# Attention scores as three fp32r passes over stored high and low parts of query and key

## The chip, the cores and the metric

The kernel runs on one core of one Trainium2 chip. The metric is the device time of one execution in microseconds (us); lower is better. TensorE is called PE, its weight loads PEld, VectorE DVE, ScalarE ACT, GpSimd POOL and SyncE SP. In this kernel nearly every DMA is issued from SP's queue, which works in order.

## The reference, cut to what matters

One layer of a decoder: a modulated norm, one input projection, two groups of heads side by side (a gated delta rule and a sparse attention), an output projection and a SwiGLU feed-forward part, for a prompt of 2048 tokens and for 8 sample rows. All arrays are float32. The part that the change touches is the prompt's sparse attention, with 4 query heads, 2 key heads and 128 channels:

```python
def block(xs):                                   # 128 queries at a time
    q_b, iq_b, iw_b, t0 = xs
    score = _index_scores(iq_b, ik, iw_b)        # 8 small indexer heads
    score = jnp.where(key_pos[None, None, :] <= qpos[None, :, None], score, -jnp.inf)
    _, idx = lax.top_k(score, topk)              # 256 keys for each query
    ...
    return _attend_selected(q_b, ks, vs, valid)  # softmax(q k / sqrt(d)) v over those keys
```

The kernel does not gather. For a block of 128 queries it forms the scores against all keys up to the block's end, adds a bias that is about -1e30 where a key was not selected, and takes the softmax over the row.

## The kernel before, in words

The work on the prompt is cut into 4 groups of 512 tokens (`g`) and 16 blocks of 128 queries (`i`). The first phase projects the four groups and runs the delta rule. The second runs the feed-forward part (`ffn`, groups 0 to 3), attention for blocks 4 to 15 (`index`, `attend`) and the sample rows (`sample_gdn`, `sample_steps`) beside each other. Blocks 0 to 3 go through `first_attn` in the first phase, in buffers that the delta rule lends.

**Two kinds of matmul.** The projections and the feed-forward part are made of `mm3`: each operand is held as a high part, rounded to the format fp32r, and a low part, the rest, and three fp32r matmuls (high by high, high by low, low by high; lines L184, L185 and L186) add up in one bank. The scores of attention (L1766) are a single matmul on float32 operands, which the trace shows as two MATMUL records. The indexer's dot products (L1721) are pairs of fp32r matmuls.

**Attention of a block.** `attend` loads the block's query `qT` once (L1755). For each of the 2 key heads and each chunk of up to 512 keys it loads `kT` (L1762), and for each of the 2 query heads it makes one score matmul into a bank of the tag `s` (two banks in all). One DVE instruction (L1767) adds the bias, keeps the running maximum and frees the bank. A block `i` has `(i+1)*128` keys, so the chunks of the 16 blocks over the 4 heads make 160 score matmuls: 112 of 512 columns and 16 each of 384, 256 and 128. Then come the exponential on ACT, transposes (L1795), products with V (L1783) and a store.

**Where query and key come from.** `tok` turns a projected block by PE transposes (L990 for the query, L1004 for the key) into a bank `s`; ACT copies it to a tile `qo` (L996, 512 columns; L1014, 256 columns); SP stores it to `qT_d` or `kT_d` in DRAM. `qo` comes from the tag `m`, 8 buffers shared by many small tiles.

**The buffers in the second phase.** `kT` and `V` have `KR` = 3 buffers of 128x512 each, `qT` one, and the sample rows' work tiles `s2` have `S2` = 8. The last feed-forward group borrows attention's tiles for its split weights: `pair()` gives, in turn, a buffer of `wi` (`WI` = 3, both parts) and a pair of one `kT` and one `V` tile.

**What sets the order.** PE's order is written by a planner (`weave`, `step`): each stage is a generator that yields what it costs on PE, how long to wait, and which banks it uses. `MM` = 0.23 is the price of an fp32r matmul of 512 columns, `F4` = 0.88 that of a float32 one. The feed-forward part runs when the other work's spent PE time has reached `PACE` times its own progress (`share`). PE's instructions are tied together as written; those of the other engines and of SP's queue are placed by a scheduler.

Of the kernel before, what the change touches and what calls it, by code (L numbers as in the profile page):

```python
# [34 lines left out]
T = 2048  # L35
# [18 lines left out]
OB = 1  # L54
KR = 3
RB = 2
WR, WI = 2, 3
S2, S4, LATE = 8, 1044, 8000
MM, TP, F4, LAG, EARLY, PACE, GONE_BY = 0.23, 0.46, 0.88, 0.6, 3000, 463, 1e9
# [53 lines left out]
class K:  # L113
# [106 lines left out]
    def build(self):  # L220
        tc, nc = self.tc, self.nc
        with ExitStack() as es:
            self.cp = self.pool(es, "cp")
            self.dr = self.pool(es, "dr", space=bass.MemoryType.DRAM)
            self.oT_d = [self.dr.tile([8, 128, T], F32, name=x) for x in ("oTh_d", "oTl_d")]
            self.qT_d = self.dr.tile([NB, 128, H * 128], F32, name="qT_d")
            self.iqT_d = self.dr.tile([NB, 128, 8 * 128], F32, name="iqT_d")
            self.kT_d = self.dr.tile([2, 128, T], F32, name="kT_d")
            self.V_d = self.dr.tile([T, 256], F32, name="V_d")
            self.ikT_d = self.dr.tile([2, 128, T], F32, name="ikT_d")  # L230
            self.cT_d = self.dr.tile([NB, 128, 12, 128], F32, name="cT_d")
            self.gz_d = self.dr.tile([NB, 128, 512], F32, name="gz_d")
            self.ikp_d = self.dr.tile([NS // 2, 128, NPAGE, 2, 64], F32, name="ikp_d")
            self.kp_d = self.dr.tile([NS, 128, NPAGE, 256], F32, name="kp_d")
            self.vp_d = self.dr.tile([NS, 128, NPAGE, 256], F32, name="vp_d")
            self.gc_d = self.dr.tile([NG, 16, 128], F32, name="gc_d")
            self.gates = {b: self.dr.tile([D], F32, name=f"gate{b}") for b in (16, 40)}
            self.x2_d = self.dr.tile([T, D], F32, name="x2_d")
            self.ps = self.pool(es, "ps", space=PSUM)


            self.p, self.wp = self.pool(es, "p"), self.pool(es, "w")
            with ExitStack() as e1:
                self.phase1(e1)
            if self.stages < 2:
                return
            with ExitStack() as e2:
                self.phase2(e2)
# [727 lines left out]
    def tok(self, what, blk, a, rows):  # L976
# [8 lines left out]
        if what == "aq":  # L985
# [5 lines left out]
            if samp:  # L991
                nc.scalar.copy(self.qTs, pt[:, :32].rearrange("p (h n) -> p h n", h=H))
                yield 0.1, 0
                return
            q = self.m("qo")[:, :512]
            nc.scalar.copy(q, pt)  # L996
            nc.sync.dma_start(self.qT_d[blk], q)
            yield TP, 0
        elif what == "kv":
# [6 lines left out]
            if samp:  # L1006
# [5 lines left out]
                return  # L1012
            q = self.m("qo")[:, :512]
            nc.scalar.copy(q[:, :256], pt[:, :256])  # L1014
            nc.sync.dma_start(self.kT_d[:, :, tk].rearrange("h p n -> p h n"), q[:, :256].rearrange("p (h n) -> p h n", h=2))
            nc.sync.dma_start(self.V_d[tk], a[:, 256:512])
# [3 lines left out]
        else:  # L1020
# [16 lines left out]
            for b in range(2):  # L1037
# [11 lines left out]
                yield TP, 0  # L1049


    def inverse(self, NT, slot):
# [626 lines left out]
    def buffers(self):  # L1679

        p = self.p2
        one = lambda tag, w, bufs=1, dt=F32: lambda: p.tile([128, w], dt, name=tag, tag=tag, bufs=bufs)
        return dict(pool=p, kT=one("kT", 512, KR), V=one("V", 512, KR), ikT=self.ikT, qT=one("qT", 512), iqT=one("iqT", 1024), sc=one("sc", T + 18, 2),
                    bias=one("bias", T, 2, BF), big=one("big", T, 2), rl=one("rl", 512, 2),
                    PT=one("PT", 512, 2), oT=one("oT", 512, OB))

    def first_attn(self, i0):
# [4 lines left out]
        if i0:  # L1692
            for a in range(2):
                ikT.append(p.tile([128, GT], F32, name="gzc", tag="gzc", bufs=2))
                nc.sync.dma_start(ikT[a], self.ikT_d[a, :, :GT])
        B = dict(pool=p, kT=one("E"), V=one("AT"), ikT=ikT, qT=one("qe"), iqT=one("sq", 1024), sc=lambda: p.tile([128, 528], F32, name="ct", tag="ct", bufs=4),
                 bias=one("dec", 512, BF), big=one("Dm"), rl=one("decb"), PT=one("Y"), oT=one("v"))
# [52 lines left out]
    def attend(self, i, B, bias):  # L1750
        nc, p = self.nc, B["pool"]
        n = (i + 1) * 128
        chunks = self.widths(n)
        qT = B["qT"]().rearrange("p (h n) -> p h n", h=H)
        nc.sync.dma_start(qT, self.qT_d[i].rearrange("p (h n) -> p h n", h=H))  # L1755
        st = p.tile([128, 4, 8], F32, name="st", bufs=2)
        oT = B["oT"]().rearrange("p (h n) -> p h n", h=H)
        for kv in range(2):
            Ps = [B["big"]() for _ in range(2)]
            for c, w in chunks:  # L1760
                kT = B["kT"]()
                nc.sync.dma_start(kT[:, :w], self.kT_d[kv, :, c * 512:c * 512 + w])  # L1762
                for r in range(2):
                    h = kv * 2 + r
                    ps = self.ps.tile([128, 512], F32, name="s", tag="s", bufs=2)
                    self.o(nc.tensor.matmul(ps[:, :w], qT[:, h, :], kT[:, :w], start=True, stop=True))  # L1766
                    nc.vector.tensor_tensor_reduce(Ps[r][:, c * 512:c * 512 + w], ps[:, :w], bias[:, c * 512:c * 512 + w], 1.0,  # L1767
                                                   GONE if c == 0 else st[:, h, c - 1:c], OP.add, OP.max, st[:, h, c:c + 1])
                    yield F4 * w / 512, 0, dict(dve=0.2 + 0.6 * w / 512, use="s", need="s")
            for r in range(2):  # L1770
# [68 lines left out]
    def ffn(self, g):  # L1839
# [51 lines left out]
        def pair():  # L1891
            ring[0] += 1
            if ring[0] % 2:
                w = wp.tile([128, 2, 512], F32R, name="wi", tag="wi", bufs=WI)
                return w[:, 0], w[:, 1]
            return [q.tile([128, 512], F32R, name=tag, tag=tag, bufs=KR) for tag in ("kT", "V")]

# [270 lines left out]
```

## Time and profile before

| | |
|---|---|
| times of three runs | 3600.11, 3608.34, 3610.41 us; median 3608.34 |
| the profiled execution | 3607.71 us, span of its instructions 3605.8 us, mean granted clock 0.971 |
| busy, of the span | PE 93%, PEld 72%, DVE 59%, ACT 41%, POOL 16% |
| DMA | 549.60 MB, mean 152 GB/s; SP's queue 47.7% of the 16 engines' time |

A row of the groups names the line, the engine, the operation, the tiles as out<-in, the shape and the count; then, after the bar, the time in which at least one of the group ran, the mean duration of one in ns, and the engine's idle time before them with what ended it. In order of time a row is the start, the duration, the engine, the line and the tiles. A matmul's duration reaches past the start of the next, so the cost of one is read from start to start.

### The profile page before, as it was taken

How to read it: one execution, taken by the hardware profiler on the slowest of the kernel's cores; microseconds unless marked ns; L12 is line 12 of the kernel's file. 1: busy time of each engine (PE TensorE's matmuls, PEld its weight loads, DVE VectorE, ACT ScalarE, POOL GpSimd, SP SyncE). 2: the span in 40 equal slices, each digit the busy share in tenths (PEclk: the TensorE clock that was granted, in tenths of full speed). 3: DMA queues.
4: the chain of work that ended last, by engine and by line, in shares of the span. 5: the costliest groups of instructions: out<-in, count | busy, mean ns of one | idle time of the engine just before them, and what ended most of it. 6: DMA issues, size and time to landing. Idle time of an engine off the chain costs nothing.

```text
span 3605.8 us, 60166 instructions
## 1 busy us (share of the span) xinstructions
PE 3362.7 (93%) x21994; PEld 2601.9 (72%) x21994; DVE 2122.1 (59%) x4502; ACT 1472.4 (41%) x2855; POOL 593.4 (16%) x539
## 2 busy tenths in 40 slices
PE   8899989989997988999998999999899999899997
PEld 5667767767775767777766777777677777677775
DVE  5555635645743656666767655666766654554545
ACT  4333322422433333444456455454545643332323
POOL 1000001100000113222220121222112112222223
PEclk9999999999998999999999999999999999999999
DMA  8754764665686244455354344335433333522221
GB/s 287 241 185 157 224 232 145 219 221 175 212 274 212 92 143 126 140 165 164 122 200 140 119 148 152 102 105 194 138 95 108 98 102 103 181 76 82 78 83 57
DMA packets 421013, 549.60 MB, mean 152 GB/s; under 512 B 50020, under 2 KB 287817, under 8 KB 420698
## 3 DMA queue, kind: packets, MB, share of 16 engines
q1 hardware_dynamic: 420690, 545.62, 47.7%
q8 instruction: 175, 2.87, 0.3%
q14 instruction: 132, 1.08, 0.1%
q10 hardware_dynamic: 16, 0.03, 0.0%
HBM read 441.78 MB, written 122.70 MB: 157 GB/s over the span
## 4 chain that ended last, share of the span: by engine, by line
PE 53%; DVE 6%; issue 3%; ACT 2%; DMA 2%; SPq 1%; POOL 1%; DVEq 0%; ACTq 0%; POOLq 0%
PE d L184 13%; PE d L186 13%; PE d L185 12%; PE s L1721 3%; PE s L1766 3%; PE g L1783 3%; PE g L1795 1%; DVE wi L168 1%; PE g L200 1%; PE g L201 1%; DMA wr<-in_w_ffn_in_dram 1%; DMA wr<-in_w_out_dram 1%; ACT bias L1590 1%; ACT wi L167 0%; DVE ca L1857 0%
## 5 line engine op out<-in xcount | busy, mean ns | idle before, releaser
L184 PE MATMUL d<-hh,wi 128*128 128x512 f32 x1616 | 694.8, 430 | 26.5 <-DVE tm L1857 6.3
L185 PE MATMUL d<-hl,wi 128*128 128x512 f32 x1616 | 643.8, 398 | 5.3 <-DVE hl L489 5.1
L168 DVE TENSOR_TENSOR wi<-wr,wi 128x512 fp32r<-128x512 f32 x525 | 396.1, 755 | 419.6 <-ACT wi L167 413.9
L186 PE MATMUL d<-hh,wi 128*128 128x512 f32 x1616 | 643.0, 398 | 0.0
L167 ACT CAST wi<-wr 128x512 fp32r<-128x512 f32 x525 | 324.4, 619 | 702.4 <-PE d L186 396.4
L184 PEld LDWEIGHTS d<-hh,wi 128*128 128x128 f32 x1616 | 310.6, 192 | 122.4 <-issue 21.0
L185 PEld LDWEIGHTS d<-hl,wi 128*128 128x128 f32 x1616 | 311.2, 193 | 75.8 <-issue 10.1
L186 PEld LDWEIGHTS d<-hh,wi 128*128 128x128 f32 x1616 | 310.0, 192 | 69.8 <-DVE wi L168 0.4
L184 PE MATMUL d<-wi,hh 128*128 128x512 f32 x736 | 317.3, 431 | 19.1 <-DMA wi<-kept 11.5
L185 PE MATMUL d<-wi,hh 128*128 128x512 f32 x736 | 292.2, 397 | 0.4 <-DVE wi L168 0.4
L186 PE MATMUL d<-wi,hl 128*128 128x512 f32 x736 | 291.7, 396 | 0.3 <-issue 0.3
L184 PE MATMUL d<-wi,ah 128*128 128x512 f32 x616 | 263.4, 428 | 9.2 <-ACT ah L2102 5.4
L2103 POOL TENSOR_TENSOR al<-ca,ah 128x512 fp32r<-128x512 f32 x88 | 121.8, 1394 | 907.0 <-ACT ah L2102 906.8
L186 PE MATMUL d<-wi,al 128*128 128x512 f32 x616 | 245.2, 398 | 2.5 <-POOL al L2103 2.5
L185 PE MATMUL d<-wi,ah 128*128 128x512 f32 x616 | 244.2, 396 | 0.0
L1730 DVE SCALAR_TENSOR_TENSOR sc<-rl,iw,sc 128x512 f32<-128x512 f32 (+3 forms) x224 | 174.9, 781 | 75.0 <-ACT rl L1723 69.0
L1723 ACT ACTIVATE rl<-s 128x512 f32<-128x512 f32 (+3 forms) x288 | 151.4, 543 | 151.7 <-PE s L1721 127.5
L1858 POOL TENSOR_TENSOR xt<-xt,tm 128x512 f32<-128x512 f32 x96 | 141.2, 1482 | 401.3 <-DVE tm L1857 339.3
L184 PEld LDWEIGHTS d<-wi,hh 128*128 128x128 f32 x736 | 140.7, 191 | 64.1 <-DMA wi<-kept 16.2
L1590 ACT ACTIVATE bias<-sc,sv 128x640 bf16<-128x640 f32 (+11 forms) x120 | 169.9, 1416 | 35.7 <-DVE sv L1592 22.9
L1721 PE MATMUL s<-ik,iqT 128*128 128x512 f32 (+3 forms) x576 | 170.6, 392 | 9.2 <-DMA iqT<-iqT_d 4.9
L186 PEld LDWEIGHTS d<-wi,hl 128*128 128x128 f32 x736 | 140.5, 191 | 32.2 <-issue 0.3
(570 smaller groups left out, 5952.8 us busy)
## 6 DMA issues: line engine op xcount, KB each, us to landing
wi<-kept SPq DMA_DIRECT2D x168, 512.0 KB
wr<-in_w_ffn_in_dram SPq DMA_DIRECT2D x584, 128.0 KB
wr<-in_w_ffn_out_dram SPq DMA_DIRECT2D x148, 256.0 KB
kept<-wi SPq DMA_DIRECT2D x56, 512.0 KB
row<-in_w_ada_dram SPq DMA_DIRECT2D x32, 512.0 KB
wr<-in_w_in_dram SPq DMA_DIRECT2D x56, 256.0 KB
xt<-in_x_prompt_dram SPq DMA_DIRECT2D x7, 2048.0 KB
kT<-kT_d SPq DMA_DIRECT2D x54, 256.0 KB
```

What stands on the lines that cost most here:

```text
L167: nc.scalar.copy(hi, wr)
L168: nc.vector.tensor_tensor(lo, wr, hi.bitcast(F32), op=OP.subtract)
L184: self.o(nc.tensor.matmul(out, wh, xh, start=start, stop=False, **kw))
L185: self.o(nc.tensor.matmul(out, wh, xl, start=False, stop=False, **kw))
L186: self.o(nc.tensor.matmul(out, wl, xh, start=False, stop=stop, **kw))
L1590: nc.scalar.activation(c, s, AF.Sign, bias=t, accum_out=cnt)
L1721: self.o(nc.tensor.matmul(ps[:, :w], iq[:, h, :].bitcast(F32R), B["ikT"][c * 2 + a][:, :w].bitcast(F32R), start=a == 0, stop=a == 1))
L1723: nc.scalar.activation(r[:, :w], ps[:, :w], AF.Relu)
L1730: nc.vector.scalar_tensor_tensor(s, r[:, :w], iw, s, op0=OP.mult, op1=OP.add)
L1766: self.o(nc.tensor.matmul(ps[:, :w], qT[:, h, :], kT[:, :w], start=True, stop=True))
L1858: (nc.vector if soon else nc.gpsimd).tensor_tensor(xt, xt, tm, op=OP.add)
L2103: nc.gpsimd.tensor_tensor(al[b], a, ah[b].bitcast(F32), op=OP.subtract)
```

## The change

Query and key are split when they are stored, and the scores become `mm3`. `parts` takes the place of the copy in `tok`: ACT casts the bank to fp32r, DVE subtracts to get the rest, and two tiles `qo` are stored by two DMAs. `qT_d` and `kT_d` hold both parts, `attend` loads both by two DMAs, and the score is three fp32r matmuls. To make room, `kT` has 2 buffers of both parts (`RK`) in place of 3 of one, `qT` one buffer of twice the size, and `s2` 6 buffers in place of 8. The borrowed weight pair becomes one `kT` buffer, of which there are 2, where it was one `kT` and one `V`, of which there were 3. In the first phase `first_attn` takes the tags `NT` and `kd` for the low parts. The planner's cost of a score falls from `F4` to `3 * MM`.

```diff
-S2, S4, LATE = 8, 1044, 8000
+RK = 2
+S2, S4, LATE = 6, 1044, 8000
...
-            self.qT_d = self.dr.tile([NB, 128, H * 128], F32, name="qT_d")
+            self.qT_d = self.dr.tile([NB, 128, 2, H * 128], F32, name="qT_d")
...
-            self.kT_d = self.dr.tile([2, 128, T], F32, name="kT_d")
+            self.kT_d = self.dr.tile([2, 128, 2, T], F32, name="kT_d")
...
-            q = self.m("qo")[:, :512]
-            nc.scalar.copy(q, pt)
-            nc.sync.dma_start(self.qT_d[blk], q)
+            for e, q in enumerate(self.parts(pt, 512)):
+                nc.sync.dma_start(self.qT_d[blk, :, e], q)
...
+    def parts(self, pt, w):
+        nc = self.nc
+        hi, lo = [self.m("qo", F32R)[:, :w] for _ in range(2)]
+        nc.scalar.copy(hi, pt[:, :w])
+        nc.vector.tensor_tensor(lo, pt[:, :w], hi.bitcast(F32), op=OP.subtract)
+        return hi.bitcast(F32), lo.bitcast(F32)
...
-        return dict(pool=p, kT=one("kT", 512, KR), V=one("V", 512, KR), ikT=self.ikT, qT=one("qT", 512), ...
+        two = lambda tag, bufs: lambda: (lambda x: [x[:, 0], x[:, 1]])(p.tile([128, 2, 512], F32R, name=tag, tag=tag, bufs=bufs))
+        return dict(pool=p, kT=two("kT", RK), V=one("V", 512, KR), ikT=self.ikT, qT=two("qT", 1), ...
...
-        B = dict(pool=p, kT=one("E"), V=one("AT"), ikT=ikT, qT=one("qe"), ...
+        two = lambda *tags: lambda: [p.tile([128, 512], F32R, name=tag, tag=tag, bufs=2) for tag in tags]
+        B = dict(pool=p, kT=two("E", "NT"), V=one("AT"), ikT=ikT, qT=two("qe", "kd"), ...
...
-                nc.sync.dma_start(kT[:, :w], self.kT_d[kv, :, c * 512:c * 512 + w])
+                for e in range(2):
+                    nc.sync.dma_start(kT[e][:, :w].bitcast(F32), self.kT_d[kv, :, e, c * 512:c * 512 + w])
...
-                    self.o(nc.tensor.matmul(ps[:, :w], qT[:, h, :], kT[:, :w], start=True, stop=True))
+                    self.mm3(ps[:, :w], *[x[:, h * 128:(h + 1) * 128] for x in qT], *[x[:, :w] for x in kT], True, True)
...
-                    yield F4 * w / 512, 0, dict(dve=0.2 + 0.6 * w / 512, use="s", need="s")
+                    yield 3 * MM * w / 512, 0, dict(dve=0.2 + 0.6 * w / 512, use="s", need="s")
...
-            return [q.tile([128, 512], F32R, name=tag, tag=tag, bufs=KR) for tag in ("kT", "V")]
+            w = q.tile([128, 2, 512], F32R, name="kT", tag="kT", bufs=RK)
+            return w[:, 0], w[:, 1]
```

How the order of the instructions changes is shown at three places. In the changed kernel the lines are shifted: `mm3` is L185, L186 and L187 there, the weights' loads are L167, the key's loads L1773.

The first place is PE in the second phase, at block 15, second key head: `s<-kT,qT` are scores, `d<-...` the feed-forward part's matmuls. Before:

```order
L1766 MATMUL s<-kT,qT 128x512 x2
L184 MATMUL d<-hh,wi 128x512
L185 MATMUL d<-hl,wi 128x512
L186 MATMUL d<-hh,wi 128x512
L1766 MATMUL s<-kT,qT 128x512 x2
```

The same place in the changed kernel:

```order
L185 MATMUL s<-kT,qT 128x512
L186 MATMUL s<-kT,qT 128x512
L187 MATMUL s<-kT,qT 128x512
L185 MATMUL s<-kT,qT 128x512
L186 MATMUL s<-kT,qT 128x512
L187 MATMUL s<-kT,qT 128x512
L185 MATMUL d<-hh,wi 128x512
L186 MATMUL d<-hl,wi 128x512
L187 MATMUL d<-hh,wi 128x512
```

Two float32 matmuls have become six fp32r ones, and the feed-forward part's groups of three stand between the chunks as before.

The second place is SP's queue at the same block: `kT<-kT_d` are the key's loads, `wr<-...` the feed-forward weights' that stand among them. Before:

```order
L166 DMA wr<-in_w_ffn_in_dram 128x256 x8
L1762 DMA kT<-kT_d 128x512
L166 DMA wr<-in_w_ffn_in_dram 128x256 x2
L1762 DMA kT<-kT_d 128x512
L166 DMA wr<-in_w_ffn_in_dram 128x256 x2
L1762 DMA kT<-kT_d 128x512 x2
L166 DMA wr<-in_w_ffn_in_dram 128x256 x6
```

In the changed kernel:

```order
L167 DMA wr<-in_w_ffn_in_dram 128x256 x12
L1773 DMA kT<-kT_d 128x512 x4
L167 DMA wr<-in_w_ffn_in_dram 128x256 x2
L1773 DMA kT<-kT_d 128x512 x4
L167 DMA wr<-in_w_ffn_in_dram 128x256 x8
```

A chunk is two DMAs now, and the loads of two chunks stand together ahead of the weights.

The third place is DVE in the first phase, where the query of group 1 is turned; `qo` is the tile that is stored, `Dm`, `Y`, `low` and `inv` belong to the delta rule, `m` to the modulation. Before:

```order
L1093 COPY_PREDICATED Dm<-cl,g 128x256
L1102 COPY Y<-g 32x256
L426 TENSOR_TENSOR m_5187<-m_5187,s 128x512
L1114 COPY low<-g 32x8x32
L1116 COPY inv_165<-g 32x8x32
L1128 COPY inv_165<-g 64x8x64
```

In the changed kernel:

```order
L1100 COPY_PREDICATED Dm<-cl,g 128x256
L1056 TENSOR_TENSOR qo<-s,qo 128x512
L1109 COPY Y<-g 32x256
L1056 TENSOR_TENSOR qo<-s,qo 128x512
L427 TENSOR_TENSOR m_5211<-m_5211,s 128x512
L1121 COPY low<-g 32x8x32
L1123 COPY inv_165<-g 32x8x32
L1056 TENSOR_TENSOR qo<-s,qo 128x512
L1135 COPY inv_165<-g 64x8x64
```

Three of the four subtractions of this group are seen here, between the delta rule's own DVE steps.

More of the change, by code (lines that the diff above doesn't have):

```diff
@@ L1012, in tok @@
                 return
-            q = self.m("qo")[:, :512]
-            nc.scalar.copy(q[:, :256], pt[:, :256])
-            nc.sync.dma_start(self.kT_d[:, :, tk].rearrange("h p n -> p h n"), q[:, :256].rearrange("p (h n) -> p h n", h=2))
+            for e, q in enumerate(self.parts(pt, 256)):
+                nc.sync.dma_start(self.kT_d[:, :, e, tk].rearrange("h p n -> p h n"), q.rearrange("p (h n) -> p h n", h=2))
             nc.sync.dma_start(self.V_d[tk], a[:, 256:512])
@@ L1682, in buffers @@
         one = lambda tag, w, bufs=1, dt=F32: lambda: p.tile([128, w], dt, name=tag, tag=tag, bufs=bufs)
-        return dict(pool=p, kT=one("kT", 512, KR), V=one("V", 512, KR), ikT=self.ikT, qT=one("qT", 512), iqT=one("iqT", 1024), sc=one("sc", T + 18, 2),
+        two = lambda tag, bufs: lambda: (lambda x: [x[:, 0], x[:, 1]])(p.tile([128, 2, 512], F32R, name=tag, tag=tag, bufs=bufs))
+        return dict(pool=p, kT=two("kT", RK), V=one("V", 512, KR), ikT=self.ikT, qT=two("qT", 1), iqT=one("iqT", 1024), sc=one("sc", T + 18, 2),
                     bias=one("bias", T, 2, BF), big=one("big", T, 2), rl=one("rl", 512, 2),
@@ L1695, in first_attn @@
                 nc.sync.dma_start(ikT[a], self.ikT_d[a, :, :GT])
-        B = dict(pool=p, kT=one("E"), V=one("AT"), ikT=ikT, qT=one("qe"), iqT=one("sq", 1024), sc=lambda: p.tile([128, 528], F32, name="ct", tag="ct", bufs=4),
+        two = lambda *tags: lambda: [p.tile([128, 512], F32R, name=tag, tag=tag, bufs=2) for tag in tags]
+        B = dict(pool=p, kT=two("E", "NT"), V=one("AT"), ikT=ikT, qT=two("qe", "kd"), iqT=one("sq", 1024), sc=lambda: p.tile([128, 528], F32, name="ct", tag="ct", bufs=4),
                  bias=one("dec", 512, BF), big=one("Dm"), rl=one("decb"), PT=one("Y"), oT=one("v"))
@@ L1753, in attend @@
         chunks = self.widths(n)
-        qT = B["qT"]().rearrange("p (h n) -> p h n", h=H)
-        nc.sync.dma_start(qT, self.qT_d[i].rearrange("p (h n) -> p h n", h=H))
+        qT = B["qT"]()
+        for e in range(2):
+            nc.sync.dma_start(qT[e].bitcast(F32), self.qT_d[i, :, e])
         st = p.tile([128, 4, 8], F32, name="st", bufs=2)
@@ L1761, in attend @@
                 kT = B["kT"]()
-                nc.sync.dma_start(kT[:, :w], self.kT_d[kv, :, c * 512:c * 512 + w])
+                for e in range(2):
+                    nc.sync.dma_start(kT[e][:, :w].bitcast(F32), self.kT_d[kv, :, e, c * 512:c * 512 + w])
                 for r in range(2):
```

## The prediction

> **What bounds the kernel now.** I read the page's busy times first, then the stages, then the scores by stage, and then single rows in order of time. From the page:
>
> ```profile
> PE 3362.7 (93%) x21994; PEld 2601.9 (72%) x21994; DVE 2122.1 (59%) x4502; ACT 1472.4 (41%) x2855; POOL 593.4 (16%) x539
> ```
>
> PE is the busy engine. The stages show where its idle time lies; a row is the stretch and its length, then the busy time of PE, PEld, DVE, ACT and POOL, the granted clock and the DMA share:
>
> ```profile
> 600.00:1260.00 660.00, 598.45 (x5756) 468.13 (x5744) 364.94 (x1001) 220.36 (x531) 53.88 (x63) 0.95 0.61 196
> 1460.00:2000.00 540.00, 500.30 (x2211) 384.90 (x2211) 368.23 (x789) 278.05 (x525) 106.81 (x91) 0.98 0.51 155
> 2000.00:2260.00 260.00, 255.49 (x1284) 188.07 (x1283) 152.83 (x291) 139.84 (x235) 55.93 (x69) 1.00 0.46 140
> 2260.00:2600.00 340.00, 324.02 (x1438) 255.00 (x1438) 227.51 (x430) 177.68 (x307) 61.80 (x48) 0.98 0.41 131
> 2600.00:3003.00 403.00, 401.66 (x1764) 315.71 (x1763) 249.54 (x462) 201.12 (x314) 78.26 (x57) 1.00 0.34 105
> 3060.00:3606.00 546.00, 515.77 (x2242) 393.36 (x2241) 284.58 (x407) 169.74 (x321) 130.43 (x100) 0.97 0.29 93
> ```
>
> The same stretches with the score line L1766 alone (PE first; each float32 matmul is two records, so x96 is 48 matmuls; the two stretches left out have 32 and 64 records):
>
> ```profile
> 600.00:1260.00 660.00, 10.86 (x32) 5.84 (x32) 0.95 0.61 196
> 1460.00:2000.00 540.00, 40.41 (x96) 17.22 (x96) 0.98 0.51 155
> ...
> 2600.00:3003.00 403.00, 44.26 (x96) 17.89 (x96) 1.00 0.34 105
> ```
>
> Nine tenths of the scores stand where PE is busy 93 to 99.7% of the time. So time taken off PE there should reach the end.
>
> **The score itself.** Rows in order of time, PE alone, around scores and around two fp32r pairs of narrow shape:
>
> ```profile
> 2991.19 1.02 PE L1766 MATMUL s<-kT,qT 128*128 128x512 f32 x2
> 2991.65 0.80 PE L184 MATMUL d<-hh,wi 128*128 128x512 f32 x1
> 2992.28 0.39 PE L185 MATMUL d<-hl,wi 128*128 128x512 f32 x1
> 2992.51 0.39 PE L186 MATMUL d<-hh,wi 128*128 128x512 f32 x1
> ...
> 1485.02 0.40 PE L1721 MATMUL s<-ik,iqT 128*128 128x256 f32 x2
> 1485.25 0.40 PE L184 MATMUL d<-wi,ah 128*128 128x512 f32 x1
> ...
> 1369.22 0.33 PE L1721 MATMUL s<-ik,iqT 128*128 128x128 f32 x2
> 1369.39 0.45 PE L184 MATMUL d<-wi,ah 128*128 128x512 f32 x1
> 1369.67 0.40 PE L185 MATMUL d<-wi,ah 128*128 128x512 f32 x1
> ```
>
> An fp32r matmul of 512 columns starts 0.23 after the one before (2992.28 to 2992.51). From 2991.19 to 2992.28 there are 1.09 us for one score and one fp32r matmul, so the score costs 0.86. Three fp32r passes cost 3 x 0.23 = 0.69: 0.17 saved. For the narrow shapes I scale the float32 cost with the columns. With 384 columns: 0.645 before, 3 x 0.173 = 0.52 after (0.23 scaled), 0.13 saved. With 256: 0.43 before; a pair takes 0.23 (1485.02 to 1485.25), so three take 0.345, 0.085 saved. With 128: 0.215 before; a pair takes 1369.67 - 1369.22 - 0.23 = 0.22, so three take 0.33, and 0.115 is lost, since half the columns do not cost half the time there. In sum 112 x 0.17 + 16 x (0.13 + 0.085 - 0.115) = 19.0 + 1.6 = 20.6 us of PE time. Weighted by PE's busy share in the scores' stages (0.91, 0.93, 0.98, 0.95 and 0.997) it is 19.7. At the far ends, 20.6 would arrive whole, or nothing if each score were waited for anyway. I take 19.7.
>
> The Trainium skill (TensorE: Matmul & The Clock Gate, "Back-to-back issue gap") states that a stream of weight loads and matmuls sustains about 131 ns for a matmul of 512 columns. By that three passes would cost 0.39, and the change would save 136 x (0.86 - 0.39) = 64 us, an estimate from the page; the rows above disagree with it, 230 ns in just such a stream, and the measurement decides.
>
> **DVE behind the score is unchanged, and sets a pace.**
>
> ```profile
> L1767 DVE CUSTOM_DVE_ANT_0 big<-s,bias,st 128x512 f32<-128x512 f32 x60 | 44.4, 746 | 16.5 <-PE s L1766 15.8
> PE s L1766 <- DVE st L1767: 7.2, 5, 2.4
> ```
>
> DVE takes 0.75 for a head and now gets one each 0.69. The second row is PE's wait for a bank of scores, 7.2 us in 5 times. Where that wait decides, a shorter score only lengthens it: 5 x 0.17 = 0.9 us of the gain if it stays with those, all of it if every head came to wait. The order keeps feed-forward groups between the chunks, so I take 1.
>
> **The split in the projections.** ACT casts in place of copying, at the same length (0.59 for the query). DVE gets 16 subtractions of 512 columns and 16 of 256, the kind of these rows:
>
> ```profile
> L168 DVE TENSOR_TENSOR wi<-wr,wi 128x512 fp32r<-128x512 f32 x525 | 396.1, 755 | 419.6 <-ACT wi L167 413.9 <-DMA kept<-wi 1.8 <-DMA oTl_d<-ol 0.8
> L1041 DVE TENSOR_TENSOR iqs<-tk,iqs 128x256 fp32r<-128x256 f32 x32 | 13.5, 422 | 12.8 <-ACT iqs L1040 11.4 <-issue 0.9
> L996 ACT COPY qo<-s 128x512 f32<-128x512 f32 x16 | 9.4, 585 | 33.0 <-PE s L990 33.0
> ```
>
> That is 16 x 0.755 + 16 x 0.422 = 18.8 us of DVE work, in stages where DVE is busy 55% (365 of 660). It holds the bank `s` longer. The bank is asked for again by the second tile after it:
>
> ```profile
> 525.61 0.60 PE L990 MATMUL s<-cf,tk 128*128 128x128 f32 x4
> ...
> 531.22 0.66 PE L990 MATMUL s<-cf,tk 128*128 128x128 f32 x4
> ```
>
> The bank of 525.61 is next written at 531.22, 5 us after the turn, against 0.6 + 0.59 + 0.76 = 2 us that it now takes. So most of it is covered by feed-forward and projection matmuls. If the cover is gone every subtraction costs its length: 0 to 18.8, and I take 2, near the lower end because of these rows. The 32 further stores on SP stand behind the subtraction, at 0.33 us an issue (a row below); with the 96 further loads that is 42 us of a queue that waits far longer for buffers. The larger use of `m` (two tiles `qo` for one) adds nothing that I can price, so it stays inside this range.
>
> **Two buffers of `kT` in place of three.** The key's loads wait in SP's queue, and what stands behind them waits too. A row has the total, the count and the longest:
>
> ```profile
> SPq L1762 <- PE s L1766: 79.6, 44, 4.5
> SPq L166 <- DVE wi L168: 862.2, 331, 21.1
> ```
>
> With three buffers 44 of 72 loads already waited for a slot. With two, chunk c needs the slot of chunk c-2. Block 15 shows the closest spacing; after it two times from issue to landing out of the chain that ended last, for a weight's load and a sample row's, of 256 KB at most:
>
> ```profile
> 2949.86 1.88 PE L1766 MATMUL s<-kT,qT 128*128 128x512 f32 x4
> ...
> 2951.77 0.33 SPq L1762 DMA_DIRECT2D kT<-kT_d  x1
> ...
> 2954.69 1.88 PE L1766 MATMUL s<-kT,qT 128*128 128x512 f32 x4
> ...
> 1619.82 2.47 DMA wr<-in_w_ffn_in_dram
> ...
> 2161.36 4.61 DMA s<-vp_d
> ```
>
> The two heads of 2949.86 end at 2951.58 (2 x 0.86), and their slot would be needed at 2954.69: 3.1 us for two loads that take 2.5 to 4.6 plus a second issue of 0.33. So such a chunk waits 0 to 1.8 us. 24 loads of the second phase belong to third or fourth chunks, and in most the spacing is wider than here. Bounds 0 to 24 x 1.8 = 43; I take 2, as four chunks at 0.5, since the order spreads the chunks over more feed-forward groups (1.4 us between two) than stood there. What lies behind on SP are the feed-forward weights; they run ahead of PE by the 862 us that the queue waits for their own buffers. The query's second load follows the first into a buffer that is free for the length of the second head pair's products; nothing. The 28 MB more in a kernel that moves 549.6 go beside the rest.
>
> The Trainium skill (SBUF — State Buffer, "The DMA setup-cost knee") gives about 2 us plus the bytes over 436 GB/s; an estimate from the page for one 256 KB load is 2.6 us. Its rule speaks against a second small load per chunk; the trace's 2.47 agrees, and its 4.61 shows what a busy queue adds.
>
> **The smaller `s2`.** The loads of the sample rows' values no longer run ahead of their round:
>
> ```profile
> 2158.35 1.07 PE L1546 MATMUL s<-s,s 128*32 128x256 f32 x16
> 2164.70 1.06 PE L1546 MATMUL s<-s,s 128*32 128x256 f32 x12
> ```
>
> A round starts 6.3 after the last, of which 1.07 is its own, so 5.3 are left for the 4.61 above. Eight rounds at 0 to 1 us; I take 1. The last feed-forward group cycles through 5 weight pairs, not 6. PE has 12 matmuls of 0.23, so 2.8 us, for each weight, and the two `kT` buffers taken every second time leave 4 x 2.8 less one weight's own use against 0.62 + 0.76 for its split: covered, 0; if it were not, half of that stage's 74 borrowed weights at 0.3, 11.
>
> **The sum.** 3607.7 is the profiled execution (span 3605.8 and 1.9 around it; 0.6 below the median of the runs). 3607.7 - 19.7 + 1 + 2 + 2 + 1 = 3594. The planner's cheaper score also moves every later stage against the feed-forward part: attention ends about 20 of the 816 weight tiles sooner. PE's waits at the joins of the groups may fall out a few us either way; no row prices that, so it widens the range by 8 on each side.
>
> **The rivals.** *The gain stays on the way.* In 1460 to 2000 PE is idle for 40 of 540 us, mostly for DVE and ACT, and 30% of the scores stand there. If these waits take up the gain of that stage and the first phase (40%, 8 us) and the small terms come to 9 instead of 6, the time is 3605. For it speaks DVE's 368 us in that stage, against it the 99.7% of 2600 to 3003. *SP's queue decides.* The key's loads of third and fourth chunks wait for their slot with the weights behind them, and PE waits at each. It takes 13.7 / 24 = 0.6 us at each of the 24 to cancel what is left of the gain; at 1.5 us it is 3594 + 36 - 2 = 3628, near the 1.8 above. For it speak the 79.6 us of waits and the 4 loads in a row in the new order, against it that PE's waits for L1766 name DVE and no load. *The passes are no cheaper.* If fp32r matmuls on these operands ran like float32, three times 0.86 would stand for one: 136 x 1.72 = 234 more, 3842. The same operand kind in the feed-forward part runs at 0.23. *The page's 131 ns* would give 3594 - 44 = 3550.
>
> **How the numbers follow.** About 0.3% (11 us) is what a measurement can tell from no change. The forecast, 3594, has 0.58, and its own range is 3583 to 3604, so a part of it, 0.08, lies within 0.3%. The gain lost on the way has 0.25, SP's queue 0.13, the page's rate 0.03, passes no cheaper 0.01. Faster is 0.50 + 0.03 and 0.05 of the second case: 0.58; slower is 0.11 of SP's queue and 0.01: 0.12; the rest, 0.30, is the same. The range runs from 3577 (all 20.6 arrive, small terms nothing, 8 and some luck at the joins) to 3616, which holds the lost gain and the milder half of SP's queue.
>
> **What would show it.** After the change scores appear as three records whose starts are 0.23 apart, and PE's busy time falls by about 20 us at no more idle time. DVE's new line in `parts` shows 32 instructions of 0.42 and 0.76, and almost no PE wait that names it. PE waits for a load of `kT` would show the term of two buffers, up to 5 us in all; waits for `wr` between 2260 and 3003 would speak for SP's queue. A PE idle time that has grown by 10 us or more in 1460 to 2600, with DVE or ACT named, would mean the gain stayed on the way.

## The result and the profile after

The changed kernel takes 3627.49 us (median of 5 runs, 3624.36 to 3636.18) against 3608.34; the ratio is 1.0061, with a 95% interval of 1.0042 to 1.0079. By the ratio it is 22 us slower (15 to 29), where 14 us faster was forecast, and it lies outside the range of 3577 to 3616. The profiled execution, the longest of the five, took 3636.18 us, with a span of 3633.9.

The page of the changed kernel, busy times:

```profile
PE 3355.5 (92%) x22154; PEld 2628.0 (72%) x22154; DVE 2148.7 (59%) x4534; ACT 1472.0 (41%) x2855; POOL 593.1 (16%) x539
```

PE's busy time fell by 7.2 us, not by 20, and its idle time (span less busy) grew from 243.1 to 278.4 us, by 35.3. The mean granted clock fell from 0.971 to 0.966, and 0.5% of 3360 us is 17 us by estimate, of the size of the 13 us that are missing from the fall; that the slower clock is what took them is not shown. First the score itself, PE alone in order of time (most lines stand 1 to 12 later than before; the score is now L185 to L187):

```profile
2522.83 0.39 PE L185 MATMUL s<-kT,qT 128*128 128x512 f32 x1
2523.05 0.39 PE L186 MATMUL s<-kT,qT 128*128 128x512 f32 x1
2523.28 0.39 PE L187 MATMUL s<-kT,qT 128*128 128x512 f32 x1
2523.51 0.22 PE L185 MATMUL s<-kT,qT 128*128 128x128 f32 x1
...
2523.79 0.45 PE L185 MATMUL d<-wi,hh 128*128 128x512 f32 x1
```

Three passes of 512 columns take 0.68 us and three of 128 take 0.28, against the 0.69 and 0.33 of the prediction. So the work of a score came out as forecast. The stages, with the columns of the prediction's table:

```profile
600.00:1260.00 660.00, 592.60 (x5795) 465.99 (x5796) 366.42 (x1008) 217.47 (x525) 50.77 (x61) 0.96 0.63 203
1460.00:2000.00 540.00, 496.94 (x2285) 393.68 (x2284) 366.23 (x789) 278.83 (x528) 109.06 (x93) 0.98 0.55 168
2000.00:2260.00 260.00, 253.13 (x1282) 190.41 (x1282) 146.40 (x279) 136.60 (x228) 49.77 (x64) 0.99 0.49 150
2260.00:2600.00 340.00, 320.52 (x1449) 259.26 (x1448) 234.14 (x441) 179.95 (x310) 66.44 (x53) 0.96 0.46 146
2600.00:3003.00 403.00, 390.40 (x1784) 314.17 (x1783) 246.83 (x456) 203.18 (x316) 70.10 (x49) 0.99 0.37 114
3060.00:3633.00 573.00, 543.85 (x2360) 416.32 (x2359) 306.93 (x424) 174.38 (x331) 144.02 (x108) 0.97 0.29 93
```

PE's idle time (the stretch less the first number) grows by 5.9 us in the first stretch, by 3.4, 2.4 and 3.5 in the next three, and by 11.3 in 2600 to 3003, which was the fullest before (1.3 us idle). The last feed-forward group keeps its 29 us: 30.2 before. The ends of a stretch are fixed times, so later stretches do not hold quite the same work. Part of the loss stands ahead of the second phase. Its first score, before and in the changed kernel:

```profile
1461.00 0.59 PE L1766 MATMUL s<-kT,qT 128*128 128x512 f32 x1
```

```profile
1473.13 0.39 PE L185 MATMUL s<-kT,qT 128*128 128x512 f32 x1
```

These are 12 of the 28 us between the two spans. One execution of each does not tell whether the change makes them: this time lies between 1452.7 and 1473.1 us in the ten profiles of the changed kernel and its variants below, and between 1456.4 and 1469.9 in the nine of kernels without parts. PE's waits, in the whole span (us in all, times, longest):

```profile
PE s L185 <- DMA kT<-kT_d: 7.6, 2, 3.9
PE s L185 <- DVE st L1778: 7.0, 8, 2.3
PE d L185 <- ACT wi L168: 3.6, 5, 2.3
PE s L1247 <- DVE qo L1056: 1.5, 1, 1.5
```

The keys' loads are waited for in two places, where PE waited for no load of `kT` before; DVE's pace behind the scores costs what it cost (7.2 before); and the projections' subtraction is hardly waited for.

### The profile page after: what moved, and what is told of

Its sections match the earlier page's. It is cut to its first block, busy times and chain, and to the rows that moved or that the text cites. A ratio compares the mean times of both kernels' runs of the same rounds, so it can differ in the third digit from the quotient of the medians.

```text
span 3633.9 us, 60690 instructions
## 1 busy us (share of the span) xinstructions
PE 3355.5 (92%) x22154; PEld 2628.0 (72%) x22154; DVE 2148.7 (59%) x4534; ACT 1472.0 (41%) x2855; POOL 593.1 (16%) x539
## 4 chain that ended last, share of the span: by engine, by line
PE 46%; DVE 7%; issue 5%; DMA 4%; ACT 3%; SPq 1%; POOL 1%; ACTq 0%; DVEq 0%; POOLq 0%
PE d L185 11%; PE d L187 11%; PE d L186 11%; PE s L1730 3%; PE g L1794 2%; DMA wr<-in_w_ffn_in_dram 2%; DVE wi L169 1%; PE g L1806 1%; ACT bias L1597 1%; PE g L201 1%; PE g L202 1%; DMA wr<-in_w_out_dram 1%; PE s L185 1%; ACT wi L168 1%; PE s L186 1%
## 5 line engine op out<-in xcount | busy, mean ns | idle before, releaser
L185 PE MATMUL d<-hh,wi 128*128 128x512 f32 x1616 | 675.7, 418 | 32.1 <-ACT hh L489 8.6
L186 PE MATMUL d<-hl,wi 128*128 128x512 f32 x1616 | 645.8, 400 | 3.1 <-DVE hl L490 2.9
L187 PE MATMUL d<-hh,wi 128*128 128x512 f32 x1616 | 645.0, 399 | 0.0
L185 PEld LDWEIGHTS d<-hh,wi 128*128 128x128 f32 x1616 | 311.2, 193 | 113.8 <-ACT hh L489 11.0
L187 PEld LDWEIGHTS d<-hh,wi 128*128 128x128 f32 x1616 | 311.1, 193 | 70.5 <-DVE wi L169 1.3
L186 PEld LDWEIGHTS d<-hl,wi 128*128 128x128 f32 x1616 | 312.0, 193 | 65.2 <-DVE hl L490 8.0
L185 PE MATMUL d<-wi,hh 128*128 128x512 f32 x736 | 313.9, 426 | 25.5 <-DMA wi<-kept 14.2
L187 PE MATMUL d<-wi,hl 128*128 128x512 f32 x736 | 292.6, 398 | 2.1 <-issue 2.1
L186 PE MATMUL d<-wi,hh 128*128 128x512 f32 x736 | 292.5, 397 | 0.2 <-DVE wi L169 0.2
L185 PE MATMUL d<-wi,ah 128*128 128x512 f32 x616 | 256.3, 416 | 11.6 <-ACT ah L2114 4.2
L187 PE MATMUL d<-wi,al 128*128 128x512 f32 x616 | 245.2, 398 | 3.4 <-POOL al L2115 3.4
L186 PE MATMUL d<-wi,ah 128*128 128x512 f32 x616 | 244.7, 397 | 0.0
L185 PEld LDWEIGHTS d<-wi,hh 128*128 128x128 f32 x736 | 141.0, 192 | 70.8 <-DMA wi<-kept 19.2
L187 PEld LDWEIGHTS d<-wi,hl 128*128 128x128 f32 x736 | 140.8, 191 | 32.2
```

The costliest lines, as they stand in the source:

```text
L185: self.o(nc.tensor.matmul(out, wh, xh, start=start, stop=False, **kw))
L186: self.o(nc.tensor.matmul(out, wh, xl, start=False, stop=False, **kw))
L187: self.o(nc.tensor.matmul(out, wl, xh, start=False, stop=stop, **kw))
```

## The experiments

Eighteen more kernels ran. Those that were measured together shared a chip and the runs of the kernel before, and each ratio is to those runs. In us a ratio stands for that part of 3608. "Setting" is the planner's pace for attention and its cost of a score (old: F4, 0.88 us; new: 3 x MM, 0.69).

| kernel | setting | ratio | 95% interval | us |
|---|---|---|---|---|
| changed kernel | 463, new | 1.0061 | 1.0042 to 1.0079 | +22 |
| b_mm: before, planner's cost alone | 463, new | 1.0059 | 1.0041 to 1.0077 | +21 |
| a_f4: changed, planner's old cost | 463, old | 1.0040 | 1.0023 to 1.0056 | +14 |
| b_s2: before, s2 of 6 | 463, old | 0.9990 | 0.9973 to 1.0006 | -4 |
| b_parts: before, parts in projections | 463, old | 0.9989 | 0.9969 to 1.0010 | -4 |
| b_rk2: before, two kT buffers | 463, old | 1.0021 | 1.0000 to 1.0043 | +8 |
| af4_rk3: a_f4, three kT buffers, s2 of 5 | 463, old | 1.0069 | 1.0048 to 1.0090 | +25 |
| af4_one: a_f4, one DMA for both parts | 463, old | 1.0054 | 1.0034 to 1.0074 | +19 |
| a3: changed, three kT buffers, s2 of 6 | 463, new | 1.0051 | 1.0034 to 1.0068 | +18 |
| b_three: before, only the passes | 463, old | 0.9995 | 0.9977 to 1.0012 | -2 |
| b_three_mm: before, only the passes | 463, new | 1.0008 | 0.9992 to 1.0024 | +3 |
| b_one: before, one pass | 463, old | 0.9866 | 0.9845 to 0.9887 | -48 |
| a_p450: changed | 450, new | 1.0009 | 0.9989 to 1.0029 | +3 |
| a3_p450: a3 | 450, new | 1.0015 | 1.0001 to 1.0028 | +5 |
| a3_p440: a3 | 440, new | 1.0018 | 0.9999 to 1.0036 | +6 |
| b_p450: before | 450, old | 1.0035 | 1.0018 to 1.0052 | +13 |
| a_p430: changed | 430, new | 0.9977 | 0.9965 to 0.9988 | -8 |
| a3_p430: a3 | 430, new | 0.9957 | 0.9939 to 0.9976 | -16 |
| b_p430: before | 430, old | 1.0050 | 1.0031 to 1.0069 | +18 |

### The planner's cost, put back and put in alone

The changed kernel (a_f4) and the kernel before (b_mm), one line each:

```
a_f4   -  yield 3 * MM * w / 512, 0, dict(dve=...
       +  yield F4 * w / 512, 0, dict(dve=...
b_mm   -  yield F4 * w / 512, 0, dict(dve=...
       +  yield 3 * MM * w / 512, 0, dict(dve=...
```

> The changed kernel, with the planner told the old cost of a score (0.88 us for 512 columns instead of 0.69), so that it lays attention beside the feed-forward part as it did before; three passes, parts, loads and buffers stay as changed. Theory ORDER (the 46 us of waiting that the changed kernel gained over its 21 us saved come from the cheaper score moving attention against the feed-forward groups, so that joins fall worse): most of it goes, 3590 to 3605 us. Theory TRANSFERS (two buffers of kT, twice the loads, the smaller s2): nothing goes, 3620 to 3630. Theory PROJECTIONS (the split's subtractions and stores in the first phase): 3620 to 3630 as well.

> The kernel before, with float32 scores, and only the planner told the new cost of a score (0.69 us). ORDER: the waits come without the passes, 3608 + 25 to 45 = 3633 to 3653 us. TRANSFERS and PROJECTIONS: 3603 to 3613, no change.

b_mm comes to +21 us: the new arrangement costs that with the old float32 scores and nothing else changed. In its profile PE is idle for 18.2 us more than before, and 15.2 of them stand in the stretch of 2460 to 2760, where the feed-forward part goes from its second to its third group. Before, then b_mm, then the changed kernel:

```profile
2460.00:2760.00 300.00, 285.53 (x1266) 224.89 (x1265) 209.77 (x399) 170.10 (x286) 54.44 (x41) 0.98 0.44 140
```

```profile
2460.00:2760.00 300.00, 270.30 (x1161) 204.08 (x1160) 199.63 (x378) 160.20 (x269) 43.47 (x35) 0.96 0.41 132
```

```profile
2460.00:2760.00 300.00, 271.84 (x1200) 214.07 (x1199) 199.98 (x385) 163.75 (x274) 45.03 (x36) 0.95 0.46 148
```

PE is idle for 14.5, 29.7 and 28.2 us, and the clock falls from 0.98 to 0.96 and 0.95. The waits in that stretch name the rows `xt` of the next group. Before and b_mm:

```profile
PE s L485 <- ACT xt L476: 4.6, 2, 3.0
...
PE s L485 <- DVE xt L478: 1.9, 2, 1.6
```

```profile
PE s L485 <- DVE xt L478: 12.0, 1, 12.0
```

What DVE does ahead of that one wait of 12.0 us in b_mm, in order of time:

```profile
2564.55 2.02 DVE L1605 MAX8 sv<-sc 128x8 f32<-128x1792 f32 x1
...
2567.35 2.03 DVE L1609 MATCH_REPLACE8 sc<-sv,sc 128x1808 f32<-128x1808 f32 x1
...
2569.29 0.68 DVE L1857 TENSOR_TENSOR tm<-d,row 128x512 f32<-128x512 f32 x1
...
2571.69 1.08 DVE L1611 TENSOR_SCALAR bias<-sc 128x1792 bf16<-128x1792 f32 x1
...
2579.09 0.75 DVE L478 TENSOR_SCALAR xt<-xt,rnz 128x1024 f32<-128x1024 f32 x1 [2.64 <-DMA x_d<-xt]
...
2579.89 0.47 PE L485 MATMUL s<-cf,xt 128*128 128x128 f32 x1 [12.00 <-DVE xt L478]
```

L1605 to L1611 are the end of a block's selection, over 1792 columns, at 2 us for L1605 and L1609, and they stand on DVE among the steps that close the group (L1857) and scale its rows (L478). They are a part of the wait only: PE's last matmul ahead of it ends at 2567.9, and from there the selection takes 2.4 of the 12.0 us (the rest of L1609, and L1611). Most of the others are the group's own steps, two splits of weights and the 2.64 us in which L478 waits for a store of `xt`. The order gives PE no attention work in this gap: the next block's scores follow at 2596.15, behind their selection, and the DVE step behind each score reads the `bias` that L1611 writes. In the kernel before a block's products stand there:

```profile
2559.27 1.13 PE L1783 MATMUL g<-PT,V 128*128 128x256 f32 x4 [1.28 <-ACT PT L1798]
...
2563.29 0.33 PE L485 MATMUL s<-cf,xt 128*128 128x128 f32 x1 [1.58 <-DVE xt L478]
...
2570.60 1.06 PE L1795 MATMUL g<-cf,big 128*128 128x128 f32 x4
```

a_f4, at +14, shows that the arrangement is not all: with the old one back, the change still does not gain, and what comes back, 8 us of 22, is within the 9 us that the two intervals leave. The theory that the arrangement explained all is refuted.

### The smaller s2, the parts, two buffers

Each alone in the kernel before:

```
b_s2     - S2, S4, LATE = 8, 1044, 8000       + S2, S4, LATE = 6, 1044, 8000
b_parts  - nc.scalar.copy(q, pt); dma_start(qT_d[blk], q)
         + for e, q in enumerate(self.parts(pt, 512)): dma_start(qT_d[blk, :, e], q)
           (and the key alike; the scores read part 0)
b_rk2    - kT=one("kT", 512, KR)              + kT=one("kT", 512, 2)
           (and two kT tiles in the last group's pairs)
```

> The kernel before, with only the ring s2 cut from 8 to 6 buffers. TRANSFERS, where s2 is its cause: the 440 to 520 tiles' stretch loses its 22 us here too, 3620 to 3630 us. ORDER, PROJECTIONS and the prediction's term of 1 us: 3605 to 3612.

> The kernel before, with only the projections' part of the change: the high and low parts are made and stored, and the scores are still one float32 product, of the high part of query and key alone (the low part is left out of the scores). PROJECTIONS: 11 us or more of the first phase's new waits, 3617 to 3627 us. The prediction's term of 2 us, ORDER and TRANSFERS: 3606 to 3613.

> The kernel before (float32 scores, one load of 256 KB for a chunk), with only the buffers of kT cut from three to two. Theory BUFFERS (a chunk's load waits for its slot and comes late, and the weights behind it on SP too; it is what is left of the loss when the planner's old cost is kept): 3608 + 10 to 25 = 3618 to 3633 us, with PE waits that name kT or the split of a weight. Rival LOADS (it is the second load and the double bytes of each chunk, not the buffers) and the prediction's term of 2: 3606 to 3612.

In the kernel before, s2 and the parts cost nothing that can be measured. Two buffers may cost up to 16 us and may cost nothing; b_rk2 has one wait of PE for a load of `kT`, of 2.9 us, where before had none.

### Three buffers, or one load

```
af4_rk3  - RK = 2, S2 = 6, KR = 3    + RK = 3, S2 = 5, KR = 2          (on a_f4)
af4_one  - for e in range(2): dma_start(kT[e][:, :w], kT_d[kv, :, e, ...])
         + dma_start(kT[:, :, :w], kT_d[kv, :, :, ...])    (query alike; on a_f4)
a3       - RK = 2, KR = 3            + RK = 3, KR = 2
         - qT = B["qT"]()            + qT = query(0) ... qT = query(1)  (256 columns each)
```

> The changed kernel with the planner's old cost of a score (3624 us alone) and three buffers of kT; to make room V has two buffers instead of three and s2 five instead of six. BUFFERS: the waits for kT (5.1 us) and for the split of a weight (6.0) go, and with them slow-clock time behind them: 3595 to 3612 us. LOADS: 3618 to 3628, no change.

> The changed kernel with the planner's old cost of a score (3624 us alone), and in the second phase one DMA of 512 KB for both parts of a chunk or of the query in place of two. LOADS, by its count of issues on SP: 3605 to 3615 us. LOADS, by its bytes: 3620 to 3628. BUFFERS: 3618 to 3628, since the slot comes free no sooner.

> The changed kernel with three buffers of kT; the room comes from V (two buffers for three) and from the query's parts, loaded for one head pair at a time, the second pair's while the first pair's products run. s2 keeps six. The planner has the new cost and the old pace. BUFFERS: PE's waits for kT (7.6 us) and the slow clock after them go, ratio to the kernel before 1.001 to 1.004 (the changed kernel: 1.006). ORDER: the joins between 2460 and 2760 still cost their 20 us, so no less than 1.000. If neither matters: 1.005 to 1.008.

One DMA in place of two gains nothing (+19 against +14, each within 7), and PE's waits for `kT` are 10.2 us there against 5.1 in a_f4. af4_rk3 takes the waits for `kT` away and loses more elsewhere, at the five buffers of s2, in the stretch of 2000 to 2260:

```profile
PE s L1553 <- DMA s<-vp_d: 15.9, 6, 3.5
```

So six buffers of s2 cost nothing and five cost 15.9 us of waits; the test of kT is spoilt by it. a3 keeps six. Its trace has no wait of PE for `kT` in a score any more, yet it stands at +18: two buffers account for 4 us, give or take 9, and V's buffers and the query's loads changed with them. At the join it waits 10.9 us for `xt`, where the changed kernel waited 6.6, after 3.7 us for a key 73 us earlier. By these rows the join took what the keys' loads gave back.

### The passes alone, in both arrangements

```
- nc.tensor.matmul(ps[:, :w], qT[:, h, :], kT[:, :w], start=True, stop=True)
+ x, y = qT[:, h, :].bitcast(F32R), kT[:, :w].bitcast(F32R)
+ for e in range(3):                        (b_one: one pass)
+     nc.tensor.matmul(ps[:, :w], x, y, start=True, stop=True)
```

> The kernel before, with each float32 score replaced by three fp32r passes of the same query and key (the low parts are left out of the scores, so they are less exact); one load, three buffers, no parts, the planner's old cost and so the old arrangement. Theory ARRIVES (PE time taken off reaches the end, and the loads and buffers take it back): ratio 0.993 to 0.996, 20 us less. Theory STAYS (the scores' saving turns into waiting for DVE, ACT and the loads around it): 0.998 to 1.002.

> The same passes with the planner's new cost, so in the changed kernel's arrangement, still with one load, three buffers and no parts. The float32 scores had 1.0059 here. ARRIVES: 1.000. STAYS: 1.004 to 1.006. The changed kernel has 1.006 in this arrangement.

> The kernel before with one fp32r pass for a score, so 0.23 us in place of 0.86 (scores of less exactness; the low parts are left out), in the old arrangement: 112 x 0.63 and the narrower ones, about 80 us of PE time less. ARRIVES: 0.978 to 0.982. STAYS, since DVE needs 0.75 for each score and the rest waits as before: 0.988 to 0.998.

In the old arrangement the passes bring 2 us of their 20 (8 at most); in the new one, against b_mm, they bring 0.0051, 18 us, give or take 9. The profiles agree: PE's busy time in b_three is 9.7 us below that of before and its idle time 18.9 above, where b_three_mm has 27.9 less and 3.7 more than b_mm. b_one takes 112 x 0.63 + 16 x (0.47 + 0.315 + 0.105) = 85 us of PE work off and gains 48: 57%. So neither theory holds throughout: how much of a saving arrives depends on the arrangement around it. The join of b_three_mm is that of b_mm (27.6 us idle in 2460 to 2760), so its 18 us came from elsewhere. With the changed kernel's loads, buffers and parts the time is 16 us above the passes alone in the old arrangement (+14 against -2) and 19 us above in the new (+22 against +3), each within 9. That is what loads, buffers and parts cost together.

### The pace

```
- MM, TP, F4, LAG, EARLY, PACE, GONE_BY = 0.23, 0.46, 0.88, 0.6, 3000, 463, 1e9
+ ...                                                            450 / 440 / 430
```

> The changed kernel with the planner's pace for attention lowered from 463 to 450 (its total cost of attention work by the 430th tile fell with the score's cost, and the pace had stayed). ORDER (the joins between 2460 and 2760 us cost about 20 us more in the new arrangement): they come out otherwise, 3595 to 3615 us, if the old distance between attention and the feed-forward part is what mattered. If any arrangement but the tuned one loses: 3620 to 3640.

> The same with the pace at 450. If BUFFERS and ORDER are two causes that add up: pace 450 gave 1.0009 with two buffers, so here 0.996 to 0.999. If they are one (attention that stands elsewhere also waits less for its keys): 1.000 to 1.002.

> The same with the pace at 440. ORDER as a matter of distance: attention ends about as many weight tiles from the end as before, 0.994 to 0.999. ORDER as luck at each join, without a trend: anything from 0.995 to 1.006.

> The kernel before, float32 scores, with only the pace at 450 in place of 463. If the kernel before stands in an arrangement that was picked for its own costs, any other costs it: 1.003 to 1.008 (the new cost of a score alone gave 1.006). If the arrangement is not special: 0.998 to 1.002.

> The changed kernel with three buffers of kT and the pace at 430, after 1.0015 at 450 and 1.0018 at 440. If the distance between attention and the feed-forward part has a trend, attention now ends too late: 1.002 to 1.006. If each arrangement is its own draw: 0.996 to 1.006.

> The kernel before, float32 scores, with the pace at 430 in place of 463 and nothing else. If the passes' saving is what arrives at pace 430: 1.002 to 1.006 (450 gave 1.0035), so that the change is worth 20 to 35 us here. If 430 is only a better arrangement for both: 0.995 to 0.999, and the change is worth nothing to 10 us.

> The changed kernel with its two buffers of kT and the pace at 430. If the two buffers cost nothing that matters (at 463 and 450 three of them gained 0.001 or nothing): 0.995 to 0.998. If three buffers are part of the gain at 430: 0.999 to 1.003.

The kernel before loses by both other paces that it was given: +13 and +18. The changed kernel gains by them: +22, +3, -8, and with three buffers +18, +5, +6, -16. Three buffers gain nothing at 450, and in a_p430, with two, PE waits for no load of `kT` at all. At 430 the change is worth 26 us with two buffers (0.9977 against 1.0050), and a3_p430, at 0.9957, is faster than both kernels; it is the version to keep. Its join, and its waits there:

```profile
2460.00:2760.00 300.00, 285.95 (x1312) 231.74 (x1311) 212.17 (x395) 169.24 (x286) 59.44 (x44) 0.98 0.48 153
```

```profile
PE s L486 <- DVE xt L479: 2.6, 1, 2.6
```

It has 14 us of idle time and the clock of before (0.98), with a block's scores standing where b_mm waited 12.0 us. But this join does not decide the time by itself: b_p430 has 14.1 us and 0.98 there and loses 18, and a_p450, at +3, has 25.5 and 0.97.

Of the expectations at 440 and 430, those by distance missed: no gain came at 440, and at 430 more came, not less; 0.9957 also lies just below the range that was given to a draw, 0.996 to 1.006. The distance can be read from the traces, as the time from the last score to the first matmul with a borrowed weight in `kT`. Before, then a_f4, then a_p430:

```profile
3000.68 1.02 PE L1766 MATMUL s<-kT,qT 128*128 128x512 f32 x2
...
3089.69 0.39 PE L184 MATMUL d<-kT,hh 128*128 128x512 f32 x1
```

```profile
3017.66 0.39 PE L185 MATMUL s<-kT,qT 128*128 128x512 f32 x1
...
3106.51 0.39 PE L185 MATMUL d<-kT,hh 128*128 128x512 f32 x1
```

```profile
3020.28 0.40 PE L185 MATMUL s<-kT,qT 128*128 128x512 f32 x1
...
3087.69 0.39 PE L185 MATMUL d<-kT,hh 128*128 128x512 f32 x1
```

It is 89, 89 and 67 us. a_f4 has the distance of before and stands at +14; a3_p440, at 94, is near it and gains nothing; a_p430, at 67, gains 8, and b_p450, at 62, loses 13. So the distance alone does not decide either. a_f4 and a_p430 have the same passes, loads, buffers and parts and differ in the planner's cost and pace only, and they are 23 us apart, give or take 7: the order of the instructions is worth that much. What in the order makes a good one stays open. A pace that fits the cost (the cheaper score wants a slower one) and a draw of its own for each arrangement both allow these points, and so few, each 4 to 7 us wide to a side, do not tell them apart. The control at 430 keeps its own cost of a score, so that its arrangement is not quite that of the changed kernel.

## Why the prediction was wrong

**The step that failed** is the end of the sum, its only words on the order: the planner's cheaper score "moves every later stage", PE's waits at the joins "may fall out a few us either way", 8 us on each side. It measured +21 us by itself (15 to 28), and by the pace the arrangement moved the kernel before by +13 and +18. That it was said to have no price was true; that it was small was a guess, and the term is as large as the saving that was worked out so closely. The kernel before stood at a pace and a cost that are better for it than the three others that were tried with its scores; the new cost threw that away.

A second step failed with it: loads, buffers and parts were to cost 5 us. By the steps from b_mm over b_three_mm to the changed kernel the sum is 21 for the order, 18 off for the passes and 19 for the rest, +22, where the prediction had 0, 18.7 off and 5. By the steps in the old order it is 2 off for the passes and 16 for the rest, so +14, and 8 more for the new order. Each of these steps is known to 7 to 9 us, and the price of the order depends on which comes first, so they do not simply add up.

**The score, 20.6 us.** Right as work: 0.68 and 0.28 us for three passes. Wrong as time: 19.7 was to arrive, and alone in the old arrangement 2 did (in the new 18). Weighting by PE's busy share says nothing about this: it gave nearly what came in the new arrangement and ten times what came in the old one. The fullest stage shows the second; before, PE was idle there for 1.3 of 403 us. In b_three, the stage and two of PE's waits in 2600 to 3060:

```profile
2600.00:3003.00 403.00, 393.79 (x1792) 319.74 (x1791) 253.91 (x461) 199.73 (x314) 78.95 (x57) 1.00 0.35 105
```

```profile
PE d L184 <- ACT wi L167: 2.7, 2, 1.9
PE d L184 <- DVE ca L1859: 2.1, 2, 1.9
```

The 48 scores of that stage are 48 x 0.17 = 8.2 us shorter, and PE is idle for 9.2 us in place of 1.3: the saving has turned into waits, the largest for the split of weights on ACT and for DVE. That the longer scores had just covered these is what the rows suggest; it was not tried by itself. b_one's 57% is a third value, and no one share holds.

**DVE's pace, +1.** 7.0 us in 8 waits against 7.2 in 5: no more than was allowed.

**The split, +2.** b_parts measures -4 (-11 to +4), and PE waits for its line in 1.8 us in all. Right, as far as this can be told. The rows of the changed kernel, minimum, median and longest ns:

```profile
L1055 ACT CAST qo<-s x32: 363/472/588, 233.1 to 1125.1; 128x512 fp32r<-128x512 f32 x16, 128x256 fp32r<-128x256 f32 x16
...
L1056 DVE TENSOR_TENSOR qo<-s,qo x32: 379/560/693, 233.7 to 1125.5; 128x512 fp32r<-128x512 f32 x16, 128x256 fp32r<-128x256 f32 x16
```

**Two buffers, +2 (0 to 43).** Within its bounds, and probably too small: b_rk2 measures +8 (0 to 16), which does not exclude 2, but the waits for `kT` were 7.6 us where up to 5 was allowed, and the one of them that is shown below has 3.0 us of slow matmuls behind it. The row of 2.47 us that the prediction set beside a load of 256 KB is one of 128 KB (`wr`, 128x256), so it says less about a key's load than was made of it. On SP the waits for a slot come to no more than before in sum:

```profile
SPq L1773 <- PE s L187: 73.8, 42, 8.1
```

42 loads wait 73.8 us for a slot, against 44 and 79.6 before, at twice the number of loads; the longest wait is 8.1 us against 4.5.

**s2, +1, and the weight pairs, 0.** Both right: b_s2 at -4 (-10 to +2), and PE idle for 29.2 us in the last group, 30.2 before.

Loads, buffers and parts were put at 5 us together, and came to 16 and 19. One by one s2, parts and buffers make 0 (-4, -4, +8, each within 8, so 13 for the sum). Whether something is left that none of them has alone is therefore not shown, though 16 and 19 speak for it. The double bytes of a chunk were not tried by themselves, and this part stays open.

**The rivals.** The time that was given to *SP's queue decides*, 3628, was met within 1 us, but not by its mechanism: the waits for `kT` are 7.6 us and not 36, no wait of PE names `wr`, and three buffers, which end the waits for `kT`, leave 3608 x 1.0051. That is luck. A time that agrees is no evidence for its mechanism. *The gain stays on the way* is what b_three shows, and stopped at 3605, a gain of 3; it had no way to a loss, since it took the arrangement as it was. Its sign did not show in the changed kernel: from 1460 to 2600 PE's idle time grew by 9.3 us where 10 was asked, and the waits that name DVE or ACT there went from 58 to 56 us, while those for `kT` are 7.6. In 2600 to 3003 they did grow. A rate of 131 ns and passes no cheaper are both excluded by the rows of 0.23.

## What to carry to other kernels

Where a planner weaves two streams by costs, a change of cost is a change of arrangement: run the old code with the new cost and the new code with the old one before the change itself is judged, and look for the pace again, since the same edit gave +22 us at one pace and -8 at another. A share of busy time does not say what part of a saving arrives; look at each join of the stages for what covers it, and ask whether that cover still stands there, but do not judge an arrangement by one join. Price a wait of PE of 2 us or more above its length, for the clock behind it.

## What the hardware showed

**A wait of PE costs more than its length.** After the changed kernel's wait of 3.68 us for a key:

```profile
2514.99 0.77 PE L185 MATMUL s<-kT,qT 128*128 128x512 f32 x1 [3.68 <-DMA kT<-kT_d]
2515.57 0.79 PE L186 MATMUL s<-kT,qT 128*128 128x512 f32 x1
2516.16 0.63 PE L187 MATMUL s<-kT,qT 128*128 128x512 f32 x1
2516.59 0.63 PE L185 MATMUL d<-wi,ah 128*128 128x512 f32 x1
...
2520.86 0.51 PE L186 MATMUL d<-wi,ah 128*128 128x512 f32 x1
2521.20 0.40 PE L187 MATMUL d<-wi,al 128*128 128x512 f32 x1
2521.44 0.39 PE L185 MATMUL d<-wi,ah 128*128 128x512 f32 x1
```

The granted clock in a slice of 2 us behind it (stretch, length, busy time of PE, PEld, DVE, ACT and POOL, clock, DMA share, GB/s):

```profile
2516.00:2518.00 2.00, 2.00 (x6) 1.52 (x6) 1.52 (x6) 1.04 (x1) 0.00 (x0) 0.50 0.62 213
```

From 2514.99 to 2521.20 there are 14 matmuls, first 0.58 and then 0.43 us apart, where 14 x 0.23 = 3.2 us would do: 3.0 us more, and none of it counted as a wait of PE. The wait of 3.68 cost 6.7. In eight of the traces (before, changed, b_mm, b_s2, a_f4, a_p450, b_p430 and a3_p430), 24 of PE's waits of 2 us or more between 1460 and 3060 us stood alone (at most 0.4 us of other idle time in the 7 us ahead and 0.5 in the 8 behind). Behind 22 of them the matmuls lost another 1.5 us or more, 3.2 at most; behind some 170 lone waits of 0.2 to 1.5 us, 4 at most did. The prediction priced every wait at its length.

The Trainium skill (TensorE: Matmul & The Clock Gate, Part 1: The HAM clock gate) says that the matmul clock falls to half after an idle window of about 3.4 us and comes back after as long a busy one, and gives 427 ns between starts of 512 columns at half rate. The 0.43 us and the 0.50 of these rows agree; the length of the window does not, since 14 of the 22 waits were shorter than 3.4 us.

**A stall with no releaser.** In 14 of 20 profiles, the changed kernel's among them, PE stops for 5.3 to 9.7 us in the middle of a run of 64 small matmuls near 615 us. The changed kernel, then before, where the nearest pause is one of 1.16:

```profile
612.33 0.38 PE L1099 MATMUL g<-Dm,Y 32*32 32x32 f32 x23 [1.05 <-DVE Dm L1095]
621.57 0.79 PE L1099 MATMUL g<-Dm,Y 32*32 32x32 f32 x41 [8.85 <-issue]
```

```profile
614.40 0.18 PE L1113 MATMUL g<-Dm,Y 32*32 32x32 f32 x1 [1.16 <-issue]
```

All eleven kernels that store the parts have it, but three of the nine others too (b_one, b_p450, b_p430), so it does not take the parts to make it; that they make it likelier is not excluded. What it waits for no view shows. b_parts has it at 8.47 us and is no slower than before, so that it seems to be made good within the first phase; that was not tried by itself.
